# Four projections accumulated side by side while the input arrives, and four edits of order, in a layer of S5 and retention heads on one core

## The chip, the core and the metric

The kernel runs on one of the eight cores of a Trainium2 chip. The core has five engines that run side by side and meet at semaphores: TensorE (PE in the profile; its weight loads are PEld), VectorE (DVE), ScalarE (ACT), GpSimd (POOL), and SyncE (SP), which here issues almost all DMA transfers. Each engine works through its own list of instructions in the order in which the program put them there. The metric is the device time of one execution in microseconds (us), the median of several runs.

## The reference, cut to what matters

One layer of a decoder works on 256 prompt positions and 8 samples of 8 positions, 320 columns in all. Everything is float32.

```
h = rms_norm(x, norm_mix)                      # x: 320 x 2048
u, q, k, v, g = split(h @ w_in)                # five parts of 1024 columns
s5_out = glu(gelu(s5_scan(u)))                 # 64 groups of 16 channels, complex states
o = retention(rotary(q), rotary(k), v)         # 8 heads of 128
ret_out = silu(g) * group_norm(o)
x = x + concat(s5_out, ret_out) @ w_out
h2 = rms_norm(x, norm_ffn)
gate, up = split(h2 @ w_ffn_in)                # 2 x 5632 columns
x = x + (silu(gate) * up) @ w_ffn_out
y = rms_norm(x, norm_final)
```

The last states of the S5 scan and of the retention are outputs too.

## The kernel before

**Products.** All large products are tiles of 128 x 128 weights (the stationary operand) by 128 x 320 of the transposed input, summed in a PSUM tile of 128 x 320. For precision a weight tile `raw` is split into `hi` (ScalarE casts it, line 130) and `lo` = `raw` - `hi` (VectorE subtracts, line 131), and the input likewise into `xhi` and `xlo`. Each tile then takes three matmuls, `hi` by `xhi`, `hi` by `xlo`, `lo` by `xhi` (lines 141 to 143). `wload` loads weights eight tiles at a time (512 KB a DMA). A product over 2048 inputs is 16 tiles, 48 matmuls and two such loads. `raw`, `hi` and `lo` have three buffers each (in the pool `wp`; later `wp2` has four of `raw`, three of the others), so a load waits until the product three loads back has let go of its buffers.

**The front.** `x` arrives in parts of 2 to 4 of its 16 tiles while two of the 40 projections of `w_in`, u0 and u1, are summed (lines 813 to 858): `py0` and the first half of `pb0` hold their sums. Then come q and k of head 0 (`gemm("ps_p", w_in[8], ...)` into the second half of `pb0`, `proj(9)` into a tile of the pool `ps_acc`), then v. The norm of x isn't needed for these sums: it is applied where PSUM is read, by the factor `rbc`. `square_x` adds the squares of x, `finish_norm` turns the sum into `rbc`, scales the rotary tables `csr` by it, and reads out u0 and u1. The pool `ps_acc` has two tiles: a projection there waits until the one before the last has been read.

**The order.** PE and POOL run in the order in which the program is written. A clock of estimated PE time, `clk.now`, decides where a generator's next piece goes: every product advances it, `spawn` puts a piece after a delay of the table `DL` (for the chunk c of the S5 part at `T0 + PER * c`), and `run_due` emits pieces when they are due. The order on DVE, ACT and SP is set by the framework's scheduler when the program is built; `tc.high_priority(offset=...)` puts instructions forward there (`EVAC` is 1500).

**Heads and chunks.** Behind the projections run the 8 heads of retention (`head_k`: `pst` transposes k, `pss` holds the scores, VectorE multiplies them by the mask into `sm` and `smp`; `head_v`: `po` is the output, then `psr`, then `pn`) and the 8 chunks of the S5 part (`s5_chunk`: transposes `pt`, products `pb`, `pk_` and `py`). VectorE computes the S5 parameters (`s5_params`, tiles `tab`, `ecs`, `lp`) in small instructions in the first 75 us. Then come w_out, the GLU, and the feed-forward part (`ffn_in`, `ffn_out`); in the first quarter of it the retention states of the samples are updated: `states_split` copies parts of `kv` to other partitions with 16 DMAs (lines 1046 to 1055), `states_load` builds a masked product `vm` on VectorE, `states_add` multiplies on TensorE (`psu`, line 1073).

Of the kernel before, what the change touches and what calls it, by code (L numbers as in the profile page):

```python
# [12 lines left out]
F32 = mybir.dt.float32  # L13
F32R = mybir.dt.float32r
# [6 lines left out]
P = 128  # L21
# [20 lines left out]


@with_exitstack
def hybrid_kernel(ctx, tc, xT, w_in, w_out, w_glu, w_fi, w_fo, vecs, s5p, bc, x0,
                  r0, trig, masks, kdec, bmask, gq,
                  yT, s5p_o, s5s_o, rp_o, rs_o):
    nc = tc.nc
# [6 lines left out]
    def f(t):  # L55
        return t.bitcast(F32)
# [18 lines left out]
    def v(nm, i):  # L75
        return vec[:, voff[nm] + i:voff[nm] + i + 1]
# [186 lines left out]
    last_ins = {}

    def split_x(c, i0, i1):
        xr = xrs[c]
        for i in range(i0, i1):
            k = 4 * c + i
            if k == 0 or c == 3 and i % 2:
                ts(xhi[:, k], xr[:, i], v("g_mix", k), MUL)  # L270
            else:
                a_ = act.mul(xhi[:, k], xr[:, i], v("g_mix", k))
                last_ins["act"] = a_
            last_ins["dve"] = dve.scalar_tensor_tensor(xlo[:, k], xr[:, i], v("g_mix", k), f(xhi[:, k]), MUL, SUB)

    def square_x():
        for xr in xrs:
            act.activation(xr, xr, AF.Square)
        a = retp[:, 0:4]
        tt(a, a, retp[:, 4:8], ADD)  # L280
        tt(u32[:, 0:4], u32[:, 0:4], u32[:, 4:8], ADD)
        tt(a, a, u32[:, 0:4], ADD)
        tt(a[:, 0:2], a[:, 0:2], a[:, 2:4], ADD)
        tt(a[:, 0], a[:, 0], a[:, 1], ADD)
        return a[:, 0]

# [214 lines left out]
    def s5_chunk(c):  # L501
# [57 lines left out]
                    mm(0.04, pb[gs, u, NC * i:NC * i + NC], bst[us, i, gs], kst[us, 2 * (i % 2) + g],  # L559
                       start=True, stop=True, tile_position=(64 * u, 64 * g))  # L560
        pk_ = misc("pk_")
        for i in range(2):
            for q in range(2):

                mm(0.12, pk_[:, 64 * i:64 * i + 64], bl[:, q, i].rearrange("p u e h -> p (u e h)"),
                   cl[:, q, i::2, 0], start=q == 0, stop=q == 1)
        for u in range(2):
            for g in range(2):
                hs = slice(16 * g, 16 * g + 16)
                act.copy(kbd[64 * g:64 * g + 64, 2 * u:2 * u + 2, hs],  # L570
                         pk_[64 * u:64 * u + 64, 0:P].rearrange("p (i u h) -> p u i h", u=2, h=32)[:, u, :, hs])
# [222 lines left out]
    def do_g(h):  # L794
        ps = proj(11 + 4 * h)
        sg = mp.tile([P, N], F32, name="sg", tag="sg", bufs=2)
        with tc.high_priority(offset=EVAC):
# [16 lines left out]
    ws = [[], []]
    with tc.high_priority(offset=100000):
        with tc.manual_schedule(engines={mybir.EngineType.SP}):
            act.dma_start(vec, vecs)
            k0 = 0
            for b, k1 in enumerate((2, 4, 8, 12, 16)):
                c, q = k0 // 4, slice(k0 % 8, (k1 - 1) % 8 + 1)  # L820
                for i in range(2):
                    if k0 % 8 == 0:
                        raw = (wp.tile([P, 8, P], F32, name="raw", tag="raw", bufs=wpool[1][0]) if not c else
                               s5.tile([P, 8, P], F32, name="raw0", tag="bst", bufs=1) if not i else
                               mp.tile([P, 8, P], F32, name="raw1", tag="rt", bufs=1))
                        ws[i].append([raw] + [wp.tile([P, 8, P], F32R, name=n, tag=n, bufs=wpool[1][1])
                                              for n in ("hi", "lo")])
                xs = [slice(0, 1), slice(1, 2)] if not b else [slice(k0 % 4, (k1 - 1) % 4 + 1)]
                for i in range(2):
                    if i < len(xs):  # L830
                        sp.dma_start(xrs[c][:, xs[i]], xT[:, 4 * c + xs[i].start:4 * c + xs[i].stop])
                    sp.dma_start(ws[i][-1][0][:, q], w_in[i, :, k0:k1])
                if b == 2:
                    sp.dma_start(prm, s5p)
                for i in range(2):
                    raw, hi, lo = ws[i][-1]
                    if i < len(xs):
                        split_x(c, xs[i].start, xs[i].stop)
                    act.copy(hi[:, q], raw[:, q])
                    last_ins["lo"] = dve.tensor_tensor(lo[:, q], raw[:, q], f(hi[:, q]), SUB)  # L840
                k0 = k1
# [6 lines left out]
    for k0, k1 in ((0, 2), (2, 4), (4, 8), (8, 12), (12, 16)):
        for i, ps in enumerate((ps0, ps1)):
            for k in range(k0, k1):  # L850
                hi, lo = (t_[:, k % 8] for t_ in ws[i][k // 8][1:])
                pe.matmul(ps, hi, xhi[:, k], start=k == 0, stop=False)
                pe.matmul(ps, hi, xlo[:, k], start=False, stop=False)
                pe.matmul(ps, lo, xhi[:, k], start=False, stop=k == KT - 1)
                clk.now += 0.4
# [187 lines left out]
    SU = {}  # L1043

    def states_split():
        kvh, kvl = (wp.tile([P, 8, P], F32R, name=n, tag=n, bufs=3) for n in ("hi", "lo"))
        act.copy(kvh, kv)
        tt(kvl, kv, f(kvh), SUB)
        SU["k"] = [wp.tile([P, 8, P], F32R, name="hi", tag="hi", bufs=3) for _ in range(2)]
        SU["v"] = [wp.tile([P, 8, P], F32R, name="lo", tag="lo", bufs=3) for _ in range(2)]  # L1050
        for i in range(2):
            for a in range(4):
                d = slice(32 * a, 32 * a + 32)
                sp.dma_start(f(SU["k"][i][d]), f((kvh, kvl)[a // 2][64 + 32 * i:96 + 32 * i]))
                sp.dma_start(f(SU["v"][i][d]), f((kvh, kvl)[a % 2][32 * i:32 * i + 32]))
# [91 lines left out]
def _host(inp):  # L1147
# [91 lines left out]
```

## Time and profile before

| | |
|---|---|
| median of 3 runs | 1469.57 us (1468.65 to 1471.67) |
| the profiled execution | 1472.44 us, its span 1470.7 us |
| mean granted TensorE clock in it | 0.991 of full speed |
| PE, PEld, DVE, ACT, POOL busy | 98%, 97%, 58%, 41%, 7% of the span |
| PE's first matmul of a product, and its last of all | 4.73 us, 1460.2 us |

The profile is of one execution. All times below are us from the start of its span. A row of the timeline gives the start, the duration, engine, line, operation, the tiles written and read, and in brackets the idle time of the engine just before, with what ended it. Matmuls are pipelined, so that the distance of two starts tells more than the duration. PEclk is the share of the full clock of 2.4 GHz that was granted in a stretch: 1.00 or, at 1.2 GHz, 0.50.

### The profile page before, as it was taken

The numbers are of one execution on the slowest core, as the hardware profiler recorded it, in microseconds if no ns is written. First come the engines' busy times: TensorE is split into PE (matmuls) and PEld (weight loads), VectorE is DVE, ScalarE is ACT, GpSimd is POOL, SyncE is SP. The second block draws the span as 40 slices with busy tenths as digits, with TensorE's granted clock in tenths as the row PEclk, the third lists the DMA queues.
The fourth block names the chain that finished last, engine by engine and source line by source line (L and its number), as shares of the span: only waits on it lengthen the run. The fifth ranks groups of instructions, "written<-read, shape, count | busy, mean of one in ns | idle before, by whom it ended". The sixth has DMA issues, their size and how long they took to land.

```text
span 1470.7 us, 26250 instructions
## 1 busy us (share of the span) xinstructions
PE 1447.6 (98%) x10590; PEld 1430.7 (97%) x10590; DVE 851.3 (58%) x1411; ACT 606.2 (41%) x972; POOL 103.2 (7%) x228
## 2 busy tenths in 40 slices
PE   9999999999999999999999999999999999999997
PEld 8899999899999999999999999999999999999996
DVE  8987776777756755665444444444444444444454
ACT  6455555455445543333333333333333333333352
POOL 2424403200000000000000000000000000000001
PEclk9999999999999999999999999999999999999999
DMA  7445554454644475665444345444445544445543
GB/s 271 153 143 165 164 161 147 140 157 142 223 144 154 148 232 174 210 215 176 154 144 157 123 145 178 151 151 147 136 142 154 167 155 146 149 123 154 152 144 112
DMA packets 85001, 235.39 MB, mean 160 GB/s; under 512 B 16400, under 2 KB 32912, under 8 KB 84880
## 3 DMA queue, kind: packets, MB, share of 16 engines
q1 hardware_dynamic: 84736, 233.68, 50.3%
q8 instruction: 84, 1.38, 0.4%
q14 instruction: 37, 0.30, 0.1%
q10 hardware_dynamic: 144, 0.04, 0.0%
HBM read 222.63 MB, written 8.95 MB: 157 GB/s over the span
## 4 chain that ended last, share of the span: by engine, by line
PE 69%; DVE 1%; DMA 0%; issue 0%; ACT 0%; DVEq 0%; SPq 0%
PE ps_fu L143 7%; PE ps_fo L143 7%; PE ps_fo L141 7%; PE ps_fu L141 7%; PE ps_fu L142 7%; PE ps_fo L142 7%; PE ps_fg L141 7%; PE ps_fg L143 7%; PE ps_fg L142 7%; PE ps_o L142 1%; PE ps_o L141 1%; PE ps_o L143 1%; PE ps_g L142 1%; PE ps_g L143 1%; PE ps_g L141 1%; DMA raw<-w_fi 0%
## 5 line engine op out<-in xcount | busy, mean ns | idle before, releaser
L131 DVE TENSOR_TENSOR lo<-raw,hi 128x1024 fp32r<-128x1024 f32 (+1 forms) x420 | 472.7, 1126 | 391.6 <-ACT hi L130 390.8
L130 ACT CAST hi<-raw 128x1024 fp32r<-128x1024 f32 (+1 forms) x420 | 406.5, 968 | 700.7 <-PE ps_fo L142 189.2
L141 PE MATMUL ps_fg<-hhi,hi 128*128 128x320 f32 x704 | 218.3, 310 | 0.0
L142 PE MATMUL ps_fg<-hlo,hi 128*128 128x320 f32 x704 | 218.0, 310 | 0.0
L143 PE MATMUL ps_fg<-hhi,lo 128*128 128x320 f32 x704 | 218.0, 310 | 0.0
L142 PE MATMUL ps_fo<-alo,hi 128*128 128x320 f32 x704 | 217.5, 309 | 0.0
L143 PE MATMUL ps_fo<-ahi,lo 128*128 128x320 f32 x704 | 217.5, 309 | 0.0
L141 PE MATMUL ps_fo<-ahi,hi 128*128 128x320 f32 x704 | 217.5, 309 | 0.0
L143 PE MATMUL ps_fu<-hhi,lo 128*128 128x320 f32 x704 | 217.4, 309 | 0.0
L142 PE MATMUL ps_fu<-hlo,hi 128*128 128x320 f32 x704 | 217.4, 309 | 0.0
L141 PE MATMUL ps_fu<-hhi,hi 128*128 128x320 f32 x704 | 217.4, 309 | 0.0
L141 PE MATMUL ps_p<-xhi,hi 128*128 128x320 f32 x576 | 183.4, 318 | 1.2 <-DVE k__3504 L176 1.2
L142 PE MATMUL ps_p<-xlo,hi 128*128 128x320 f32 x576 | 178.9, 311 | 0.0
L143 PE MATMUL ps_p<-xhi,lo 128*128 128x320 f32 x576 | 178.9, 311 | 0.0
L142 PEld LDWEIGHTS ps_fg<-hlo,hi 128*128 128x128 f32 x704 | 133.0, 189 | 0.4
L141 PEld LDWEIGHTS ps_fg<-hhi,hi 128*128 128x128 f32 x704 | 132.9, 189 | 0.3
L143 PEld LDWEIGHTS ps_fg<-hhi,lo 128*128 128x128 f32 x704 | 133.0, 189 | 0.0
L142 PEld LDWEIGHTS ps_fu<-hlo,hi 128*128 128x128 f32 x704 | 132.4, 188 | 0.0
L143 PEld LDWEIGHTS ps_fu<-hhi,lo 128*128 128x128 f32 x704 | 132.4, 188 | 0.0
L141 PEld LDWEIGHTS ps_fu<-hhi,hi 128*128 128x128 f32 x704 | 132.4, 188 | 0.0
L141 PEld LDWEIGHTS ps_fo<-ahi,hi 128*128 128x128 f32 x704 | 132.1, 188 | 0.0
L142 PEld LDWEIGHTS ps_fo<-alo,hi 128*128 128x128 f32 x704 | 132.1, 188 | 0.0
(404 smaller groups left out, 1966.7 us busy)
## 6 DMA issues: line engine op xcount, KB each, us to landing
raw<-w_fi SPq DMA_DIRECT2D x176, 512.0 KB, 3.7
raw<-w_in SPq DMA_DIRECT2D x76, 512.0 KB, 4.2
raw<-w_fo SPq DMA_DIRECT2D x64, 512.0 KB, 3.5
raw<-w_out SPq DMA_DIRECT2D x32, 512.0 KB, 3.8
raw<-w_fo SPq DMA_DIRECT2D x64, 192.0 KB, 2.4
rt<-r SPq DMA_DIRECT2D x8, 512.0 KB, 5.4
raw<-w_glu SPq DMA_DIRECT2D x8, 512.0 KB, 3.5
raw<-r SPq DMA_DIRECT2D x8, 512.0 KB, 4.4
```

The source lines that it names most:

```text
L130: act.copy(hi[:, :m], raw[:, :m])
L131: dve.tensor_tensor(lo[:, :m], raw[:, :m], f(hi[:, :m]), SUB)
L141: pe.matmul(ps, hi, xhi[:, k], start=k == 0, stop=False)
L142: pe.matmul(ps, hi, xlo[:, k], start=False, stop=False)
L143: pe.matmul(ps, lo, xhi[:, k], start=False, stop=k == nk - 1)
```

## The change

Four outputs (u0, u1, and q and k of head 0) are summed at once while x comes in. Their weights stand in one new array `w_in4`, in which a tile k of x finds its four weight tiles side by side: a DMA of 512 KB brings the weights of all four for two tiles of x. `x` comes in parts of 1, 1, and then 2 tiles; its squares are taken part by part between the casts. The other edits: `pk_` is computed in eight matmuls of 64 x 32 outputs instead of four of 128 x 64, the three mask products of `head_k` get the priority `EVAC`, `states_split` as a whole gets the priority 6000, and the table has `nm` 0.8 instead of 7.8 (the norm's delay) and `T0` 54.6 instead of 52.6.

```diff
-    def square_x():
-        for xr in xrs:
-            act.activation(xr, xr, AF.Square)
...
+    def square_x(k0, k1):
+        xr = xrs[k0 // 4][:, k0 % 4:(k1 - 1) % 4 + 1]
+        act.activation(xr, xr, AF.Square)
...
-        for i in range(2):
-            for q in range(2):
-
-                mm(0.12, pk_[:, 64 * i:64 * i + 64], bl[:, q, i].rearrange("p u e h -> p (u e h)"),
-                   cl[:, q, i::2, 0], start=q == 0, stop=q == 1)
+        for u in range(2):
+            for i in range(2):
+                for q in range(2):
+                    mm(0.04, pk_[64 * u:64 * u + 64, 32 * i:32 * i + 32],
+                       bl[:, q, i, u].rearrange("p e h -> p (e h)"), cl[:, q, 2 * u + i, 0],
+                       start=q == 0, stop=q == 1, tile_position=(0, 64 * u))
...
-        tt(sm[:, 0:256], pss[:, 0:256], mk[:, 0:NP], MUL)
-        tt(sm[:, 256:384], pss[:, 256:384], mk[:, 0:P], MUL)
-        tt(smp[64:128, :, 0:NS], pss[64:128, 384:448].rearrange("p (b t) -> p b t", t=NS),
-           mk[64:128, NP:320].rearrange("p (b t) -> p b t", t=NS), MUL)
+        with tc.high_priority(offset=EVAC):
+            tt(sm[:, 0:256], pss[:, 0:256], mk[:, 0:NP], MUL)
+            tt(sm[:, 256:384], pss[:, 256:384], mk[:, 0:P], MUL)
+            tt(smp[64:128, :, 0:NS], pss[64:128, 384:448].rearrange("p (b t) -> p b t", t=NS),
+               mk[64:128, NP:320].rearrange("p (b t) -> p b t", t=NS), MUL)
...
-              o=2.2, u=6.0, c=10.0, n2=2.4, n2b=2.6, nm=7.8)
-    T0, PER = 52.6, 34.0
+              o=2.2, u=6.0, c=10.0, n2=2.4, n2b=2.6, nm=0.8)
+    T0, PER = 54.6, 34.0
...
+    pk0 = ps_acc.tile([P, 512], F32, name="ps_p", tag="acc", bufs=2)
+    accs = [py0[:, :N], pb0[:, 0, :N], pb0[:, 1, :N], pk0[:, :N]]
...
+    for k1 in (1, *range(2, KT + 1, 2)):
+        with tc.high_priority(offset=100000), tc.manual_schedule(engines={mybir.EngineType.SP}):
+            if k0 % 2 == 0:
+                raw, hi, lo = (wp.tile([P, 8, P], d, name=n, tag=n, bufs=3).rearrange("p (k o) m -> p k o m", o=4)
+                               for n, d in (("raw", F32), ("hi", F32R), ("lo", F32R)))
+            q = slice(k0 % 2, (k1 - 1) % 2 + 1)
+            sp.dma_start(xrs[k0 // 4][:, k0 % 4:(k1 - 1) % 4 + 1], xT[:, k0:k1])
+            sp.dma_start(raw[:, q], w_in4[:, k0:k1])
...
+            split_x(k0, k1)
+            act.copy(hi[:, q], raw[:, q])
+            last_lo = dve.tensor_tensor(lo[:, q], raw[:, q], f(hi[:, q]), SUB)
...
+        if k1 % 2 == 0:
+            accq = square_x(k1 - 2, k1)
+        for k in range(k0, k1):
+            for w_, x_ in ((hi, xhi), (hi, xlo), (lo, xhi)):
+                for i, ps in enumerate(accs):
+                    pe.matmul(ps, w_[:, k % 2, i], x_[:, k], start=k == 0 and w_ is hi and x_ is xhi,
+                              stop=k == KT - 1 and w_ is lo)
+            clk.now += 1.6
+        k0 = k1
+    ps0, ps1, pq, pk = accs
...
-    pq = gemm("ps_p", w_in[8], KT, xhi, xlo, ps=pb0[:, 1, :N])
-    pk = proj(9)
...
     def states_split():
+
+        with tc.high_priority(offset=6000):
+            states_split_()
+
+    def states_split_():
...
+    A["w_in4"] = c(A["w_in"][[0, 1, 8, 9]].transpose(1, 2, 0, 3))
```

Three places show how the built order moves. The first is TensorE's list from the first product on; `py` and the two halves of `pb` are three of the sums, `ps_p` in the changed list is the fourth. Before:

```order
L116 MATMUL warm_ps<-ones 128x512 x8
L852 MATMUL py_259<-xhi,hi 128x320
L853 MATMUL py_259<-xlo,hi 128x320
L854 MATMUL py_259<-xhi,lo 128x320
L852 MATMUL py_259<-xhi,hi 128x320
L853 MATMUL py_259<-xlo,hi 128x320
L854 MATMUL py_259<-xhi,lo 128x320
L852 MATMUL pb_260<-xhi,hi 128x320
```

and in the changed kernel:

```order
L116 MATMUL warm_ps<-ones 128x512 x8
L846 MATMUL py_152<-xhi,hi 128x320
L846 MATMUL pb_153<-xhi,hi 128x320 x2
L846 MATMUL ps_p<-xhi,hi 128x320
L846 MATMUL py_152<-xlo,hi 128x320
L846 MATMUL pb_153<-xlo,hi 128x320 x2
L846 MATMUL ps_p<-xlo,hi 128x320
L846 MATMUL py_152<-xhi,lo 128x320
L846 MATMUL pb_153<-xhi,lo 128x320 x2
L846 MATMUL ps_p<-xhi,lo 128x320
```

A tile of x now gives twelve matmuls in a row on four sums, where it gave three on one. The sums of squares (`ps_r`) come after k has been summed, two tiles into v, where they came four tiles into k.

The second is VectorE's list where head 0's q and k have been rotated: `k_<-ps_p,csr` reads the PSUM tile of k, `sg<-ps_p,rbc` reads that of g, the projection after v. Before:

```order
L176 TENSOR_TENSOR q__766<-q__766,sw 128x320
L176 TENSOR_TENSOR ecs<-tab 128x3x32
L180 SCALAR_TENSOR_TENSOR ecs<-ecs 128x3x32
L176 TENSOR_TENSOR tab<-ecs 128x64 x2
L180 SCALAR_TENSOR_TENSOR ecs<-ecs 128x2x32
L176 TENSOR_TENSOR ecs<-tab 128x2x32
L176 TENSOR_TENSOR tab<-tab 128x32
L131 TENSOR_TENSOR lo<-raw,hi 128x1024
L176 TENSOR_TENSOR k__774<-ps_p,csr 128x320
L176 TENSOR_TENSOR sw<-sw,csr 128x320
L170 TENSOR_SCALAR tab<-tab 128x32 x2
L176 TENSOR_TENSOR k__774<-k__774,sw 128x320
```

and in the changed kernel:

```order
L176 TENSOR_TENSOR q__786<-q__786,sw 128x320
L176 TENSOR_TENSOR ecs<-tab 128x3x32
L176 TENSOR_TENSOR sg<-ps_p,rbc 128x320
L180 SCALAR_TENSOR_TENSOR ecs<-ecs 128x3x32
L176 TENSOR_TENSOR tab<-ecs 128x64
L131 TENSOR_TENSOR lo<-raw,hi 128x1024
L176 TENSOR_TENSOR k__794<-ps_p,csr 128x320
L176 TENSOR_TENSOR sw<-sw,csr 128x320
L176 TENSOR_TENSOR tab<-ecs 128x64
L176 TENSOR_TENSOR k__794<-k__794,sw 128x320
```

The read of g's sum stood right behind the last row of k; now it stands ahead of the read of k's sum, with a `lo` between them.

The third is VectorE's list at the first pair of feed-forward products: `fg` and `fu` read the sums of gate and up, `hi<-lo,bmk` and `lo<-lo,bmk` build `vm` for the states of heads 0 and 1, `lo<-raw,hi` are the weights. Before:

```order
L176 TENSOR_TENSOR fg<-ps_fg,rbc_5869 128x320
L131 TENSOR_TENSOR lo<-raw,hi 128x1024
L176 TENSOR_TENSOR fu<-ps_fu,rbc_5869 128x320
L176 TENSOR_TENSOR fu<-fu,fg 128x320
L131 TENSOR_TENSOR lo<-raw,hi 128x1024
L176 TENSOR_TENSOR alo<-fu,ahi 128x320
L131 TENSOR_TENSOR lo<-raw,hi 128x1024
```

and in the changed kernel:

```order
L176 TENSOR_TENSOR fg<-ps_fg,rbc_5921 128x320
L176 TENSOR_TENSOR fu<-ps_fu,rbc_5921 128x320
L176 TENSOR_TENSOR fu<-fu,fg 128x320
L176 TENSOR_TENSOR alo<-fu,ahi 128x320
L176 TENSOR_TENSOR hi<-lo,bmk 128x512 x2
L176 TENSOR_TENSOR lo<-lo,bmk 128x512 x2
L131 TENSOR_TENSOR lo<-raw,hi 128x1024 x3
L176 TENSOR_TENSOR fg<-ps_fg,rbc_5921 128x320
```

The `lo` of the second half of the next gate weights stood ahead of `fu`; now it stands behind `alo` and the four builds. On SP the 16 DMAs of `states_split` stood one by one between weight loads; now they stand in one block behind the third `raw<-w_fi` of `wp2`, and the load of that same second half is the first one behind the block.

## Rows read from the trace of the kernel before

**Rows 1.** Waits of PE: line, waited for, us in total, times, longest

```profile
PE psu L1073 <- issue: 2.7, 1, 2.7
PE po L102 <- DVE smp L176: 2.0, 1, 2.0
...
PE ps_p L141 <- DVE k__3504 L176: 1.2, 1, 1.2
...
PE po L102 <- DVE lp L176: 0.9, 1, 0.9
PE pst L107 <- DVE k__3504 L176: 0.8, 1, 0.8
...
PE pss L102 <- ACT kbd L570: 0.5, 1, 0.5
```

**Rows 2.** Stretches: length, busy us (instructions) of PE to POOL, PEclk, DMA share, GB/s

```profile
7.60:11.00 3.40, 3.40 (x15) 3.40 (x14) 1.67 (x4) 1.42 (x4) 0.39 (x3) 0.50 0.92 311
40.50:57.90 17.40, 17.40 (x122) 17.40 (x121) 17.34 (x69) 9.42 (x14) 4.23 (x9) 1.00 0.54 174
65.60:72.50 6.90, 6.00 (x35) 5.39 (x36) 6.36 (x21) 1.65 (x5) 5.06 (x10) 0.51 0.37 106
577.60:581.10 3.50, 3.50 (x16) 3.50 (x15) 2.96 (x6) 0.46 (x1) 0.00 (x0) 0.51 0.41 146
```

**Rows 3.** Timeline of PE where one sum follows another

```profile
23.89 0.31 PE L854 MATMUL py<-xhi,lo 128*128 128x320 f32 x1
24.03 0.31 PE L852 MATMUL pb<-xhi,hi 128*128 128x320 f32 x1
```

**Rows 4.** Timeline of PE where v begins

```profile
40.54 0.31 PE L141 MATMUL ps_pv<-xhi,hi 128*128 128x320 f32 x1
...
40.98 0.83 PE L102 MATMUL ps_r<-ident,ry 128*128 128x128 f32 x6
41.57 0.39 PE L141 MATMUL ps_pv<-xhi,hi 128*128 128x320 f32 x1
```

**Rows 5.** Timeline of ACT in the first 19 us

```profile
5.91 0.56 ACT L272 ACTIVATE xhi<-u,vec 128x320 fp32r<-128x320 f32 x1 [1.92 <-DMA u<-xT]
...
18.45 0.60 ACT L839 CAST hi<-raw 128x512 fp32r<-128x512 f32 x1
```

**Rows 6.** Timeline of DVE, 43 to 56 us

```profile
43.17 0.89 DVE L176 TENSOR_TENSOR csr<-csr,rbc 128x320 f32<-128x320 f32 x2
...
53.39 1.22 DVE L131 TENSOR_TENSOR lo<-raw,hi 128x1024 fp32r<-128x1024 f32 x1
54.52 0.48 DVE L176 TENSOR_TENSOR k__774<-ps_p,csr 128x320 f32<-128x320 f32 x1
```

**Rows 7.** Timeline of PE, the transposes of head 0

```profile
57.94 0.49 PE L107 MATMUL pst<-ident,k__774 128*128 128x128 f32 x3
...
81.93 0.60 PE L107 MATMUL pn<-ident,on 128*128 128x128 f32 x4
```

**Rows 8.** The page's DMA issues: count, KB each, median us to landing

```profile
raw<-w_fi SPq DMA_DIRECT2D x176, 512.0 KB, 3.7
```

**Rows 9.** Timeline of SP's queue, the first DMA of `states_split`

```profile
525.45 0.60 SPq L1054 DMA_DIRECT2D hi<-hi  x1
```

**Rows 10.** Timeline of DVE in the first feed-forward products

```profile
531.74 0.49 DVE L176 TENSOR_TENSOR fu<-ps_fu,rbc 128x320 f32<-128x320 f32 x1 [1.38 <-PE ps_fu L143]
...
533.81 0.48 DVE L176 TENSOR_TENSOR alo<-fu,ahi 128x320 fp32r<-128x320 f32 x1
...
576.66 1.29 DVE L176 TENSOR_TENSOR lo<-lo,bmk 128x512 fp32r<-128x512 f32 x2
```

**Rows 11.** Timeline of PE, one S5 chunk's small products

```profile
131.73 0.78 PE L102 MATMUL pb<-kst,bst 64*64 64x80 f32 x32
132.44 1.10 PE L102 MATMUL pk__1772<-cl,bl 128*128 128x64 f32 x8
133.36 0.39 PE L141 MATMUL ps_p<-xhi,hi 128*128 128x320 f32 x1
```

More of the change, by code (lines that the diff above doesn't have):

```diff
@@ L44, in hybrid_kernel @@
 @with_exitstack
-def hybrid_kernel(ctx, tc, xT, w_in, w_out, w_glu, w_fi, w_fo, vecs, s5p, bc, x0,
+def hybrid_kernel(ctx, tc, xT, w_in, w_in4, w_out, w_glu, w_fi, w_fo, vecs, s5p, bc, x0,
                   r0, trig, masks, kdec, bmask, gq,
@@ L261, in hybrid_kernel, with split_x @@
     xrs = [u32[:, 0:4], u32[:, 4:8], retp[:, 0:4], retp[:, 4:8]]
[L263 to L270, printed above, removed]
-            else:
-                a_ = act.mul(xhi[:, k], xr[:, i], v("g_mix", k))
-                last_ins["act"] = a_
-            last_ins["dve"] = dve.scalar_tensor_tensor(xlo[:, k], xr[:, i], v("g_mix", k), f(xhi[:, k]), MUL, SUB)
-    def square_x():
-        for xr in xrs:
-            act.activation(xr, xr, AF.Square)
[L279 to L285, printed above, removed]
+    def split_x(k0, k1):
+        for k in range(k0, k1):
+            xr = xrs[k // 4][:, k % 4]
+            if k == 0:
+                ts(xhi[:, k], xr, v("g_mix", k), MUL)
+            else:
+                act.mul(xhi[:, k], xr, v("g_mix", k))
+            dve.scalar_tensor_tensor(xlo[:, k], xr, v("g_mix", k), f(xhi[:, k]), MUL, SUB)
+    def square_x(k0, k1):
+        xr = xrs[k0 // 4][:, k0 % 4:(k1 - 1) % 4 + 1]
+        act.activation(xr, xr, AF.Square)
+        if k1 == 8:
+            tt(u32[:, 0:4], u32[:, 0:4], u32[:, 4:8], ADD)
+        elif k1 == 12:
+            tt(u32[:, 0:4], u32[:, 0:4], retp[:, 0:4], ADD)
+        elif k1 > 12:
+            a = u32[:, 0:2]
+            tt(a, a, u32[:, 2:4] if k1 == 14 else retp[:, 6:8], ADD)
+            if k1 == 14:
+                tt(a, a, retp[:, 4:6], ADD)
+            else:
+                tt(a[:, 0], a[:, 0], a[:, 1], ADD)
+        return u32[:, 0]
     NE = 8
@@ L570, in s5_chunk @@
                 act.copy(kbd[64 * g:64 * g + 64, 2 * u:2 * u + 2, hs],
-                         pk_[64 * u:64 * u + 64, 0:P].rearrange("p (i u h) -> p u i h", u=2, h=32)[:, u, :, hs])
+                         pk_[64 * u:64 * u + 64, 0:64].rearrange("p (i h) -> p i h", h=32)[:, :, hs])
         pvs = [pb[:, u, 0:4 * NC].rearrange("p (r q t) -> p r q t", r=2, q=2) for u in range(2)]
@@ L812, in hybrid_kernel @@
     act.activation(warm, ones[:, 0:1], AF.Silu)
[L814 to L841, printed above, removed]
@@ L842, in hybrid_kernel @@
-    with tc.issue_after(last_ins["lo"].ins):
-        dt_ = s5_step()
     py0 = ps_y.tile([P, 512], F32, name="py0", tag="y", bufs=1)
     pb0 = ps_b.tile([P, 2, 512], F32, name="pb0", tag="pb", bufs=1)
-    ps0, ps1 = py0[:, :N], pb0[:, 0, :N]
     keep_warm(8)
[L848 to L855, printed above, removed]
@@ L856, in hybrid_kernel @@
-    with tc.issue_after(last_ins["act"].ins), tc.issue_after(last_ins["dve"].ins):
-        accq = square_x()
+    pk0 = ps_acc.tile([P, 512], F32, name="ps_p", tag="acc", bufs=2)
+    accs = [py0[:, :N], pb0[:, 0, :N], pb0[:, 1, :N], pk0[:, :N]]
+    with tc.high_priority(offset=100000), tc.manual_schedule(engines={mybir.EngineType.SP}):
+        act.dma_start(vec, vecs)
+    k0 = 0
+    for k1 in (1, *range(2, KT + 1, 2)):
+        with tc.high_priority(offset=100000), tc.manual_schedule(engines={mybir.EngineType.SP}):
+            if k0 % 2 == 0:
[4 more added lines that the diff above has]
+            sp.dma_start(raw[:, q], w_in4[:, k0:k1])
+            if k1 == 6:
+                sp.dma_start(prm, s5p)
+            split_x(k0, k1)
+            act.copy(hi[:, q], raw[:, q])
+            last_lo = dve.tensor_tensor(lo[:, q], raw[:, q], f(hi[:, q]), SUB)
+        if k1 == 6:
+            with tc.issue_after(last_lo.ins):
+                dt_ = s5_step()
+        if k1 % 2 == 0:
+            accq = square_x(k1 - 2, k1)
+        for k in range(k0, k1):
+            for w_, x_ in ((hi, xhi), (hi, xlo), (lo, xhi)):
[4 more added lines that the diff above has]
+        k0 = k1
```

## The prediction, made before the changed kernel ran

> **What bounds the kernel now.** The page's first part comes first: TensorE is busy for 98% of the span, and its clock is granted at 0.991. So only TensorE's idle time and its time at half clock can be won. One tile's three matmuls run from 40.54 to 40.98 [rows 4]: 0.147 us each, 7.04 us for a product of 48. I read the places where TensorE departs from that.
>
> The start. The first matmul of a product is at 4.73, and v begins at 40.54 [rows 4]. Between them lie 4 x 48 = 192 matmuls, 28.2 us, and the first six `ps_r`, about the 0.6 us of the second six (40.98 to 41.57). 4.73 + 28.2 + 0.6 = 33.5: 7.0 us are lost, since two sums give 96 matmuls for 16 tiles of x and x comes in slower than that. In 7.6 to 11.0 TensorE also runs at 0.50 of the clock while 311 GB/s come in [rows 2].
>
> The list of waits [rows 1] gives the rest: `po` waits for `smp` (2.0) and `lp` (0.9) at 63 to 66.5; `pss` 0.5 at 98.8; a projection and `pst` wait for a rotated k (1.2 and 0.8) at 268; `psu` 2.7, ending at 576.84, put down to "issue", where the program's order shows `hi`, `lo` and `vm` of the states as what it needs.
>
> A wait costs more than itself. After the `po` waits the clock is 0.51 for 6.9 us, after `psu` 0.51 for 3.5 us [rows 2]: 3.4 and 1.7 us of TensorE's time. I take the same 1.7 behind the two waits at 268, 2.0 together, and none behind the 0.5 at 98.8.
>
> Last, VectorE. From 40.5 to 57.9 it is busy 17.34 of 17.40 us [rows 2]: there an end moves only by what stands in its list.
>
> **A. Start to the first `pn`.** *The sums.* Tile 0 gives twelve matmuls from about 4.73. Tile 1 of x and its four weight tiles (416 KB together) come behind it; before, two tiles of x with their weights were the unit. `xhi` of tile 1 waited for its DMA until 5.91 [rows 5]. The weights for it are 256 KB in place of 128 KB a tile for two tiles; with 311 GB/s I set their landing 0.9 later, about 7.0, and the cast of 128x512 adds 0.60 [rows 5]: 7.65. Twelve at half clock, 24 x 0.147 = 3.5: 11.2. From there 14 tiles x 12 x 0.147 = 24.7: the four sums end at 35.8. They need 832 KB per two tiles in 3.52 us, 242 GB/s (1 KB = 1024 bytes), below the 311 that the trace shows. ScalarE's share of two tiles (casts, `xhi`, squares) is some 2.7 us, VectorE's some 3.1, both under 3.5; so the moved squares and casts cost nothing, and some 0.8 and 0.4 us in each 3.5 if that cover failed, 6 and 3 us in all. Before, the same point is 40.54 less 0.6 of `ps_r` inside, 39.9: 4.1 earlier.
>
> *The read of k.* The new order spends some of it. `ps_r` comes two tiles into v, at 36.7, the second `ps_r` fourteen tiles into it, at 42.3; before, the second was at 40.98 and `csr` at 43.17 [rows 4, 6]. So `csr` comes at about 44.5, later than before. From there to the end of k's read I count in VectorE's list 7 reads or products of 128x320 at 0.40, two `csr` at 0.40, some 15 small ones at 0.15 and three `lo` at 1.13 (53.39 to 54.52 [rows 6]), with gaps 9.7: 54.1. TensorE has done v, two `ps_r` and g by 35.8 + 7.0 + 1.2 + 7.0 = 51.0, and u2 needs the tile that held k. It waits 3.1 us. The least is 2.4: the read of `sg` needs the end of g, and behind it come two small ones (0.3), `lo` 1.13 and k's read 0.48, whenever the sums end. The most I take is 4.1, with `csr` one us later. Half a clock follows, 1.7. Before, k's read began at 54.52, ahead of the read of g, and TensorE did not wait.
>
> *Then to `pn`.* u2 from 54.1 gives 18 matmuls (2.6) + 1.7 until `pst` at 58.4; it was at 57.94 [rows 7]. From there to `pn` at 81.93 it took 24.0. The priority puts the mask products ahead of the parameters, so the 2.9 of `po`'s waits and 3.0 of the 3.4 of half clock should go: 18.1, `pn` at 76.5. **Gain 5.4.**
>
> **B. `pss` at 98.8.** It now stands ahead of `pk_`, with `kbd` ready: **0.5**.
>
> **C. The wait at 268.** The read of k stood behind the chunk's mask products on VectorE and stands ahead of them now: 1.2 + 0.8 + 1.7 = **3.7**; nothing, if VectorE is late for another reason.
>
> **D. `states_split`.** 2.7 + 1.7 = 4.4 go. But its 16 DMAs now form one block on SP, 0.60 us each in issue [rows 9], and a load stands behind them. The first eight wait for buffers of the first gate product's first half, the others for its end. `fu` is read at 531.74 when the first up product ends [rows 10], so that gate product ended 7.0 earlier, at 524.5. 524.5 + 8 x 0.60 = 529.3; then the second half of the next gate's weights is issued, lands 3.7 later [rows 8] at 533.0, and is cast by 534.1 to 534.6. Its `lo` stands behind `fu`, `alo` (533.81 before [rows 10], 533.7 at best now) and four builds of `vm`, 1.29 for two [rows 10], 2.5 for four: 536.2, with its own 1.13 at 537.3. TensorE began that product at 531.5 and needs this `lo` 24 matmuls and two later, at 535.2. A new wait of 2.1 + 1.7 of clock: 3.8. **Net 0.6**; 4.4 if the builds find a gap, about -1 if the block issues later by 1.6.
>
> **E. `pk_`.** Eight records with 128 columns of weights take 0.92 us (132.44 to 133.36) and become sixteen with 64. `pb`'s 32 records, on a quarter of the array, take 0.71 (131.73 to 132.44) [rows 11]: 0.022 each, four side by side 0.089. Sixteen at 0.022 are 0.4, 0.5 less; at 0.089, 1.4, 0.5 more. `pk_` runs two halves side by side, between these: I take 0, with -4 to +4 us for eight chunks. The Trainium skill ("TensorE: Matmul & The Clock Gate", section "LDWEIGHTS (loading the stationary operand)") says that a load's time goes with its columns: by that sixteen loads of half the columns take what eight took, and this term would stay 0. The sum stands without it.
>
> The new `nm` and `T0` move pieces of equal work; their effect on the norm is in A. A later chunk is covered by the head products between.
>
> **The sum.** 5.4 + 0.5 + 3.7 + 0.6 + 0 = 10.2. The profiled execution takes 1472.44, so 1462.2. It is 2.9 above the median of the runs shown; I carry the difference to the median: 1469.57 - 10.2 = **1459.4**.
>
> **The rivals.** *R1: the block of D hides.* If the `lo` behind the block is in time, 3.8 more: 1455.6. For it: VectorE is nearly idle between the products there, and the cast may be early. Against it: DMA, `fu` and builds all stand ahead in fixed lists. 0.20.
>
> *R2: the wait at 268 stays, or one like it comes up in another head.* Each head reads k by the same list, and the whole order of VectorE is moved: 3.7 less, 1463.1. For it: one head of eight lost this before. 0.25.
>
> *R3: the change brings nothing.* VectorE is full to 57.9 [rows 2], and if it stays the bound until `pn`, and C stays too, 0.5 + 0.6 are left: 1468.5. Against it: what it computes behind k is moved behind the masks, not only shifted. 0.07.
>
> *R4, slower: the four sums never get the full clock.* Twelve matmuls go round over four PSUM tiles, where each tile gave its sum three in a row. If the clock then stays at half until the sums end, 168 matmuls cost 24.7 more. The wait for k drops to its least (0.7 less) and most of A's 5.4 is consumed: 10.2 - 24.7 + 0.7 + some 1.7 of a clock that can't fall further = -12; 1481 to 1482. It ends slower from about 70 matmuls at half clock on. Against it: a change of the sum from `py` to `pb` costs 23.89 to 24.03 [rows 3], 0.14, no more than within a sum. The Trainium skill (the same page, section "A second HAM failure mode: psum-queue depth-cycling") tells of a kernel whose clock went to and fro as it cycled through PSUM banks; by that rule R4 holds. The traced change of tiles speaks against it so far. 0.03.
>
> **How the numbers follow.** 0.45 for the forecast, 0.20, 0.25, 0.07, 0.03 for the rivals. The bounds of k's wait (-0.7, +1.0), of E (4 either way, likelier within 2) and of D widen each by some 2 us. From R1 less 1.6 to R2 plus 2.9: 1454 to 1466, which leaves out R3, R4 and the tails of E, under 0.2. About 0.2%, 2.9 us, is what a measurement here can tell from no change: faster below 1466.6, slower above 1472.5. Forecast, R1 and R2 lie below but for their tails (0.03), R3 within with part of these, R4 and two mishaps together above: 0.87, 0.08, 0.05.
>
> **What would show it.** A: twelve matmuls a tile at 0.147 from 11.2, v at 35.8, a wait of some 3 us for k's read at 51 to 54, `pst` near 58.4, `pn` near 76.5, no wait of `po`. C: none at 268. D: no `psu` wait; a wait for `lo` at 535, of some 2 us. E: sixteen `pk_` records in some 0.9 us. Wrong would make it: gaps between the tiles of x (the DMA or the casts are the bound), a half clock past 11.2, a wait in a later head, or a `pk_` round of 1.4 us.

## The result, and the profile after

The changed kernel takes 1474.91 us (median of 9 runs, 1474.05 to 1476.02), the kernel before 1470.78 in as many runs beside it (1468.65 to 1472.64): a ratio of 1.0030, 95% interval 1.0021 to 1.0039. It is slower by some 4 us where 10 less were forecast. The profiled execution takes 1475.36 us, 2.92 more than that of before. One of the ten executions of e1 below took 2013.88 us, and its median is that of the other nine.

The waits of TensorE after, the view of [rows 1]:

```profile
PE py L102 <- DVE xp L176: 6.2, 1, 6.2
PE ps_p L141 <- DVE sg L176: 3.2, 1, 3.2
PE py L846 <- DVE xhi L170: 3.2, 1, 3.2
PE ps_p L141 <- DVE k__3502 L176: 1.3, 1, 1.3
...
PE ps_fg L141 <- ACT hi L130: 1.1, 1, 1.1
PE ps_fg L143 <- DVE lo L131: 0.7, 1, 0.7
PE ps_p L143 <- DVE lo L131: 0.7, 1, 0.7
PE ps_p L141 <- DVE q__1098 L176: 0.5, 1, 0.5
```

Of the six waits of [rows 1] five are gone; that of a projection for a rotated k has 1.3 where it had 1.2. The two largest that no step of the prediction had are the first and the third line.

**The start.** VectorE's and GpSimd's timelines in the first 9 us:

```profile
3.29 4.69 DVE L170 TENSOR_SCALAR xhi<-u,vec 128x320 fp32r<-128x320 f32 x1 [3.29 <-DMA vec<-vecs]
8.01 0.55 DVE L270 SCALAR_TENSOR_TENSOR xlo<-u,vec,xhi 128x320 fp32r<-128x320 f32 x1
```

```profile
3.05 1.20 POOL L319 MEMSET xp<- 128x640 f32 x2
4.19 0.20 POOL L319 MEMSET kbd<- 128x128 f32 x1
4.34 1.17 POOL L319 MEMSET ush<- 128x1280 f32 x1
5.45 2.27 POOL L319 MEMSET cl<- 128x1280 f32 x2
7.65 0.11 POOL L464 MEMSET tab<- 128x8 f32 x1
7.69 0.11 POOL L465 MEMSET tab<- 128x8 f32 x1
```

The first `xhi` of VectorE takes 4.69 us and ends at 7.98, just after GpSimd's last memset (7.80). So TensorE begins at 8.13 where it began at 4.73. This row and later ones of its timeline:

```profile
8.13 0.39 PE L846 MATMUL py<-xhi,hi 128*128 128x320 f32 x1 [3.23 <-DVE xhi L170]
...
37.89 0.31 PE L141 MATMUL ps_pv<-xhi,hi 128*128 128x320 f32 x1
...
56.71 0.60 PE L141 MATMUL ps_p<-xhi,hi 128*128 128x320 f32 x1 [3.23 <-DVE sg L176]
...
60.92 0.49 PE L107 MATMUL pst<-ident,k__794 128*128 128x128 f32 x3
...
78.86 0.89 PE L107 MATMUL pn<-ident,on 128*128 128x128 f32 x3
...
375.25 2.43 PE L102 MATMUL py<-xp,cl 128*32 128x80 f32 x64 [6.23 <-DVE xp L176]
```

The four sums take 29.8 us (8.13 to 37.89). v begins 2.7 earlier than in [rows 4], `pn` comes 3.1 earlier than in [rows 7]. Up to here the change is a gain.

**The last chunk.** The last row is the loss. VectorE's list ahead of that `py`:

```profile
368.32 1.29 DVE L176 TENSOR_TENSOR v<-w,tab 128x512 f32<-128x512 f32 x2
369.53 0.48 DVE L176 TENSOR_TENSOR sg<-ps_p,rbc 128x320 f32<-128x320 f32 x1
369.94 1.22 DVE L131 TENSOR_TENSOR lo<-raw,hi 128x1024 fp32r<-128x1024 f32 x1
371.07 1.69 DVE L176 TENSOR_TENSOR r4a<-retp,r4a 128x320 fp32r<-128x320 f32 x4
372.68 0.48 DVE L176 TENSOR_TENSOR r4b<-retp,r4b 128x320 fp32r<-128x320 f32 x1
373.08 0.49 DVE L176 TENSOR_TENSOR retp<-retp,sg 128x320 f32<-128x320 f32 x1
373.48 1.29 DVE L176 TENSOR_TENSOR r4b<-retp,r4b 128x320 fp32r<-128x320 f32 x3
374.69 0.74 DVE L176 TENSOR_TENSOR xp<-v,v 128x252 f32<-128x252 f32 x2
```

`v` is ready at 369.6, but `xp`, which TensorE waits for, stands behind the splits of the heads' outputs for w_out (`r4a`, `r4b`, line 947), which TensorE needs only after that `py`. Before, `xp` stood right behind `v`, ahead of the splits:

```profile
368.17 1.29 DVE L176 TENSOR_TENSOR v<-w,tab 128x512 f32<-128x512 f32 x2
...
369.50 0.75 DVE L176 TENSOR_TENSOR xp<-v,v 128x252 f32<-128x252 f32 x2
370.16 1.22 DVE L131 TENSOR_TENSOR lo<-raw,hi 128x1024 fp32r<-128x1024 f32 x1
371.30 1.69 DVE L176 TENSOR_TENSOR r4a<-retp,r4a 128x320 fp32r<-128x320 f32 x4
```

TensorE also has less to do in between. From the chunk's `pb` to its `py` it took 12.8 us before, with 75 matmuls of projections behind `pk_`:

```profile
359.24 0.78 PE L102 MATMUL pb<-kst,bst 64*64 64x80 f32 x32
...
372.05 0.74 PE L102 MATMUL py<-ush,kbd 128*32 128x320 f32 x8
372.61 1.29 PE L102 MATMUL py<-xp,cl 128*32 128x80 f32 x64
```

In the changed kernel it takes 9.2, with 51 of them:

```profile
359.05 0.78 PE L102 MATMUL pb<-kst,bst 64*64 64x80 f32 x32
...
368.27 0.74 PE L102 MATMUL py<-ush,kbd 128*32 128x320 f32 x8
```

Within that wait the clock falls, in the view of [rows 2]:

```profile
56.70:60.00 3.30, 3.29 (x12) 3.30 (x13) 3.30 (x14) 1.15 (x3) 0.47 (x1) 0.50 0.89 259
374.10:380.80 6.70, 5.55 (x76) 5.26 (x77) 5.55 (x19) 1.47 (x3) 0.00 (x0) 0.50 0.81 304
541.50:544.90 3.40, 2.70 (x17) 2.44 (x18) 2.74 (x3) 2.10 (x2) 0.00 (x0) 1.00 0.91 347
```

TensorE is busy in 5.55 of the 6.7 us at 0.50, which costs 2.8: with the wait 9.0, nearly all of the gain that was forecast. (The expectations below take 3.4, half of the whole stretch.) The two waits for `hi` and `lo` at 541 cost no clock in this execution.

### The profile page after: what moved, and what is told of

It reads as the page before. It is cut to its first block, busy times and chain, and to the rows that moved or that the text cites. A ratio compares the mean times of both kernels' runs of the same rounds, so it can differ in the third digit from the quotient of the medians.

```text
span 1473.6 us, 26372 instructions
## 1 busy us (share of the span) xinstructions
PE 1444.0 (98%) x10654; PEld 1426.7 (97%) x10654; DVE 854.3 (58%) x1405; ACT 607.6 (41%) x973; POOL 101.8 (7%) x228
## 4 chain that ended last, share of the span: by engine, by line
PE 69%; DVE 1%; issue 0%; ACT 0%; DVEq 0%
PE ps_fo L143 7%; PE ps_fo L142 7%; PE ps_fu L143 7%; PE ps_fu L142 7%; PE ps_fu L141 7%; PE ps_fo L141 7%; PE ps_fg L143 7%; PE ps_fg L141 7%; PE ps_fg L142 7%; PE ps_o L142 1%; PE ps_o L141 1%; PE ps_o L143 1%; PE ps_g L142 1%; PE ps_g L143 1%; PE ps_g L141 1%; DVE x L176 0%
## 5 line engine op out<-in xcount | busy, mean ns | idle before, releaser
L130 ACT CAST hi<-raw 128x1024 fp32r<-128x1024 f32 (+1 forms) x416 | 402.0, 967 | 680.1 <-PE ps_fo L142 189.3
L141 PE MATMUL ps_p<-xhi,hi 128*128 128x320 f32 x560 | 178.4, 318 | 5.2 <-DVE sg L176 3.2
L143 PE MATMUL ps_p<-xhi,lo 128*128 128x320 f32 x560 | 173.9, 311 | 0.7 <-DVE lo L131 0.7
L142 PE MATMUL ps_p<-xlo,hi 128*128 128x320 f32 x560 | 173.6, 310 | 0.0
```

The costliest lines, as they stand in the source:

```text
L130: act.copy(hi[:, :m], raw[:, :m])
L143: pe.matmul(ps, lo, xhi[:, k], start=False, stop=k == nk - 1)
```

## The experiments

Theory: two causes, VectorE's `TENSOR_SCALAR` held by GpSimd's memsets at the start, and the place of `xp` behind the splits in VectorE's list. Rivals: the first is a late input; the second comes from a late VectorE; or one of the repairs (priorities, `pk_`) does harm by itself. All times below are medians with their ratio to the kernel before on the same chip.

**The start.** e1 changes the operation:

```diff
-                ts(xhi[:, k], xr, v("g_mix", k), MUL)
+                dve.scalar_tensor_tensor(xhi[:, k], xr, v("g_mix", k), ones[:, 0:1].to_broadcast([P, N]), MUL, MUL)
```

> The changed kernel, but VectorE makes xhi of tile 0 with a SCALAR_TENSOR_TENSOR (x by the factor by ones) in place of the TENSOR_SCALAR that took 4.69 us and ended when GpSimd's memsets ended. Theory (a TENSOR_SCALAR of 32 bits waits for GpSimd, the three-operand form doesn't): xhi takes about 0.55 us, the first matmul of a product comes at about 4.6 in place of 8.13, and what follows is 3.4 us earlier up to the read of sg at 56: from there VectorE decides, so that between 1 and 3.4 us reach the end, 1471.5 to 1474. Rival (VectorE is held by a late input or by every operation beside memsets): xhi still takes over 4 us, 1474.9.

1473.02 us, ratio 1.0015 (1.0006 to 1.0025). e6 keeps the operation and moves GpSimd's memsets:

```diff
-    for t_ in (*d0s, *xps, kbd, ush, *cls_):
-        pool.memset(t_, 0.0)
...
+            if k1 == 1:
+                pool.tensor_scalar(kbd[:, 0], f(xhi[:, 0, 0:32]), 0.0, None, MUL)
+                for t_ in (*d0s, *xps, kbd, ush, *cls_):
+                    pool.memset(t_, 0.0)
```

> The changed kernel with VectorE's TENSOR_SCALAR for xhi of tile 0 as it was, and GpSimd's memsets of d, xp, kbd, ush and cl behind it: a small product of GpSimd that reads xhi stands ahead of them. Theory (the memsets held the TENSOR_SCALAR): it takes 0.5 us or less in place of 4.69, the first matmul of a product comes at 4.2 to 4.8, the time as in the run with the three-operand form, 1473.2. Rival (this operation is slow there for another reason): over 3 us still, 1474.9.

1473.24 us, ratio 1.0020 (1.0011 to 1.0029). VectorE's first operation in e1:

```profile
3.44 0.55 DVE L267 SCALAR_TENSOR_TENSOR xhi<-u,vec,ones 128x320 fp32r<-128x320 f32 x1 [3.44 <-DMA vec<-vecs]
```

and in e6, the same operation as in the changed kernel:

```profile
3.37 0.39 DVE L170 TENSOR_SCALAR xhi<-u,vec 128x320 fp32r<-128x320 f32 x1 [3.37 <-DMA vec<-vecs]
```

Both ways the long wait is gone, the first product matmul is at 4.67 and 4.70, and 1.7 to 1.9 us reach the end. `pn` comes at 75.39 in e1. What held VectorE were the memsets (e6), and the operation with two tensor operands was not held beside the same memsets (e1). The Trainium skill ("SBUF — State Buffer", section "Who interferes with whom") says that a VectorE operation in a two-port mode and a GpSimd operation lock each other out for a whole instruction. The 4.69 us beside the memsets and the 0.39 without them agree with it, though no run shows in which mode the operation was; and in the changed kernel VectorE lost to memset after memset, until GpSimd had none left.

e16 puts ScalarE in VectorE's place for this tile in the kernel before:

```diff
-            if k == 0 or c == 3 and i % 2:
+            if c == 3 and i % 2:
```

> The kernel before with xhi of tile 0 by ScalarE. Theory (there too the TENSOR_SCALAR waited for GpSimd, 1.18 us in its profile where 0.39 is what it takes): the first matmul of a product 0 to 0.5 earlier; the stretch behind waits for x, so 0 to 0.7 less, and the spread of its times (1467.5 to 1474) smaller if some executions waited 4.7 us: none over 1472. Rival (no such executions before): same time, same spread.

1470.81 us, 0.9997 (0.9985 to 1.0009), times from 1467.65 to 1473.79. The rival holds: nothing is won before, and the spread there comes from elsewhere.

**The last chunk.** e2 and e9 change T0 (54.6), e3 gives `xp` of the last chunk a priority, e10 takes the old `pk_`, e13 changes its planned cost only:

```diff
-    T0, PER = 54.6, 34.0
+    T0, PER = 50.6, 34.0
```

> The changed kernel with T0 50.6 in place of 54.6, by which VectorE's list has xp of the last chunk ahead of the splits r4a and r4b again. Theory (the wait of 6.2 at 375 and the 6.8 us of half clock behind it come from that order): both go, 1474.9 - 6.2 - 3.4 = 1465.3. Rival (the chunk is late on VectorE because of the four sums or the mask products): a wait of 4 us or more stays, 1473 to 1475.

```diff
+        with (tc.high_priority(offset=EVAC) if c == 7 else ExitStack()):
             tt(xp[:, 0, :, 1:NCP], t[0][:, 0, :, 0:NCP - 1], t[1][:, 1, :, 0:NCP - 1], SUB)
             tt(xp[:, 1, :, 1:NCP], t[0][:, 1, :, 0:NCP - 1], t[1][:, 0, :, 0:NCP - 1], ADD)
```

> The changed kernel with the priority EVAC for the two products that write xp in the last chunk, nothing else; in VectorE's list they stand ahead of r4a. Theory (those splits ahead of xp are most of the wait of 6.2): xp is done at about 371.8 in place of 375.3, the wait falls to 2.8, the half clock to one stretch of 3.4 us: 1474.9 - 3.4 - 1.7 = 1469.8. Rival (what stands ahead of v, not behind it, makes it late): the wait stays over 5, 1474.9.

```diff
-    T0, PER = 54.6, 34.0
+    T0, PER = 52.6, 34.0
```

> The changed kernel with T0 52.6, as it was before the change. Its list on VectorE still has the second product of xp behind r4a and r4b, though the last chunk now begins 15 matmuls of projections earlier. Theory (the place of xp in VectorE's list is what counts): a wait of 5 to 6.2 stays at 375, 1474 to 1475. Rival (the two us of T0 are the cause): the wait goes, 1465 to 1468.

```diff
-        for u in range(2):
-            for i in range(2):
-                for q in range(2):
-                    mm(0.04, pk_[64 * u:64 * u + 64, 32 * i:32 * i + 32],
...
+        for i in range(2):
+            for q in range(2):
+                mm(0.12, pk_[:, 64 * i:64 * i + 64], bl[:, q, i].rearrange("p u e h -> p (u e h)"),
...
```

> The changed kernel with pk_ in four matmuls of 128 x 64 again, at their old cost in the planner's clock; T0 stays 54.6. By that cost the last chunk stands 3 matmuls earlier, and VectorE's list has both products of xp ahead of r4a. Theory (place in the list): the wait at 375 falls to about 2.6, half clock to one stretch, as with the priority for xp: 1469.8, with 0.6 more for pk_ itself (0.92 us a chunk in place of 0.84): 1470.4. Rival (pk_ has nothing to do with it): 1474.9 to 1475.5.

```diff
-                    mm(0.04, pk_[64 * u:64 * u + 64, 32 * i:32 * i + 32],
+                    mm(0.06, pk_[64 * u:64 * u + 64, 32 * i:32 * i + 32],
```

> The changed kernel with one number changed: the planned cost of each of the eight pk_ matmuls 0.06 in place of 0.04, so that a chunk's pk_ costs 0.48 in the planner's clock, as in the kernel before. TensorE's list then has the last chunk where the run with the old pk_ has it (54 matmuls ahead of py), but VectorE's list still has the second product of xp behind r4b. Theory (the place of xp in VectorE's list sets the wait): a wait of 3 us or more at the last py stays, 1472 to 1474. Rival (the chunk's place on TensorE does, or the form of pk_ cost the time): the first gives 1466.2 as with the old pk_, the second 1474.9.

| run | us | ratio (95%) | waits at the last `py` |
|---|---|---|---|
| e2, T0 50.6 | 1466.57 | 0.9963 (0.9949 to 0.9977) | none |
| e3, `xp` first | 1469.80 | 0.9994 (0.9985 to 1.0004) | 2.6 |
| e9, T0 52.6 | 1473.80 | 1.0023 (1.0014 to 1.0033) | 1.1 + 3.1 |
| e10, old `pk_` | 1466.84 | 0.9972 (0.9961 to 0.9983) | 0.6 |
| e13, cost 0.06 | 1473.08 | 1.0013 (1.0003 to 1.0022) | 1.1 + 4.7 |

e3 came out at its forecast: nothing but the place of `xp` is changed there, and 5 us come back. e2 is 1.3 slower than its theory. e9 is just below its range, with 4.2 of wait where 5 to 6.2 were expected. e10 is 3.6 faster than its theory, which had a wait of 2.6 left. e13 is the sharpest: TensorE's list has the chunk where e10 has it, but VectorE's list still has the second product of `xp` behind `r4b`:

```profile
366.50 0.41 DVE L176 TENSOR_TENSOR xp<-v,v 128x252 f32<-128x252 f32 x1
...
370.38 1.29 DVE L176 TENSOR_TENSOR r4b<-retp,r4b 128x320 fp32r<-128x320 f32 x3
371.58 0.41 DVE L176 TENSOR_TENSOR xp<-v,v 128x252 f32<-128x252 f32 x1
```

and the wait stays, where in e10 both stand ahead:

```profile
364.35 0.74 DVE L176 TENSOR_TENSOR xp<-v,v 128x252 f32<-128x252 f32 x2
365.00 1.22 DVE L131 TENSOR_TENSOR lo<-raw,hi 128x1024 fp32r<-128x1024 f32 x1
366.14 1.70 DVE L176 TENSOR_TENSOR r4a<-retp,r4a 128x320 fp32r<-128x320 f32 x4
```

TensorE's rows there, of e13 and then of e10:

```profile
367.06 0.35 PE L102 MATMUL py<-xp,cl 128*32 128x80 f32 x8 [1.07 <-DVE xp L176]
372.14 2.10 PE L102 MATMUL py<-xp,cl 128*32 128x80 f32 x56 [4.74 <-DVE cl L176]
```

```profile
364.90 1.51 PE L102 MATMUL py<-xp,cl 128*32 128x80 f32 x64 [0.62 <-ACT r4a L945]
```

In both, 54 matmuls stand between `pk_` and `py`, and `py` comes 9.7 us after `pb`; the wait is 5.8 in e13 and 0.6 in e10. So the list on VectorE makes that difference. The profile puts 4.7 of e13 and 3.1 of e9 down to `cl`, the row behind `xp` in that list, and the 0.6 of e10 to `r4a`; but TensorE goes on 0.14 us after the `xp` that it needs has ended each time (372.00 to 372.14, 372.52 to 372.66, 364.76 to 364.90).

TensorE's side counts beside it. e3 has the list right and keeps the 51 matmuls, and a wait of 2.6 and a stretch of half clock stay. Of the 24 matmuls that the changed kernel lacks there, T0 takes 15 (e9 has 66) and the planned cost of `pk_` 3 (e13); the other 6 are not assigned.

Which edit turned VectorE's list is not shown. The old T0 alone (e9) and the old planned cost alone (e13) leave the second product of `xp` behind the splits; T0 50.6 (e2) or the old `pk_` with its old cost (e10) puts both ahead. e2, e10 and e13 had the short start in their profiles (`xhi` 1.17, 1.19 and 1.28 us), so some 2 us of their times beside the changed kernel may be the start.

**The start and the last chunk together.** e5 is e2 with `act.mul` for tile 0, e15 is e10 with it:

```diff
-            if k == 0:
-                ts(xhi[:, k], xr, v("g_mix", k), MUL)
-            else:
-                act.mul(xhi[:, k], xr, v("g_mix", k))
+            act.mul(xhi[:, k], xr, v("g_mix", k))
```

> The changed kernel with T0 50.6 and with xhi of tile 0 made by ScalarE like all others. Theory (two separate causes, the start and the last chunk): their gains add up, 1466.6 less 1.7 to 3.4, so 1463.2 to 1464.9. Rival (what is won at the start is lost again at the read of sg and k, which VectorE's list sets): 1466.6.

1465.03 us, 0.9962 (0.9948 to 0.9977): just above the theory's range and 1.5 below e2, but the ratios of the two are the same (0.9963 in e2), so that a gain over e2 is not shown.

> The changed kernel with the old pk_ and xhi of tile 0 by ScalarE: both causes taken away with T0 54.6 left. The run with the old pk_ alone had the short start in its profile (first matmul before 5 us, xhi 1.19 us) and times from 1463.9 to 1468.3. Theory (VectorE's TENSOR_SCALAR waits in some executions and not in others): without it the times stay in the lower half, median 1464 to 1465.5, none over 1467. Rival (that spread comes from elsewhere): 1466.8, up to 1468.

1465.09 us, 0.9952 (0.9937 to 0.9967), 1463.49 to 1465.57, where e10 had 1463.92 to 1468.32. That the upper half of e10's times were long starts fits, with 4 times against 7; it was not traced run by run.

**The repairs by themselves.** e4 is the changed kernel, and e7 is e5, without the priority of `states_split`; e11 is e5 without that of the mask products:

```diff
-        with tc.high_priority(offset=6000):
-            states_split_()
+        states_split_()
```

> The changed kernel without the priority 6000 of states_split. Theory (it took away the wait of 2.7 and half clock of 1.7 at psu and put waits of 1.1 and 0.7 for hi and lo at 541 in their place): psu waits again, those go, 1474.9 + 4.4 - 1.8 = 1477.5. Rival (psu no longer waits, since its pieces stand at other places now): 1473.1.

> As the run with T0 50.6 and xhi by ScalarE, and without the priority 6000 of states_split. Theory (with the priority, hi and lo of the second gate product come late, which cost 2.3 + 0.5 of waits and 3.4 of half clock in the run with T0 50.6, more than the wait of 2.7 and 1.7 at psu that it takes away): 1.7 less than its neighbour, 1461.5 to 1463. Rival (my forecast: the priority is worth 0.6): 0.6 more than its neighbour or above.

e4 takes 1474.75 (1.0025, 1.0015 to 1.0034), e7 1465.15 (0.9963, 0.9949 to 0.9977): as their neighbours, between the two forecasts each time. In both traces `psu` waits 2.7 again and the waits for `hi` and `lo` of the second gate product are gone. The priority exchanges one for the other.

```diff
-        with tc.high_priority(offset=EVAC):
+        if True:
             tt(sm[:, 0:256], pss[:, 0:256], mk[:, 0:NP], MUL)
...
```

> As the run with T0 50.6 and xhi by ScalarE, and without the priority of the three mask products. Theory (that priority took away the waits of po for lp and smp, 2.9, and 3.4 of half clock): they come back, 1465.0 + 3 to 6.3 = 1468 to 1471.3. Rival (VectorE had done the parameters by then anyway, since TensorE comes later relative to it): 1465.0.

1463.22 us (0.9953, 0.9937 to 0.9970), not slower than e5, and `po` waits for nothing. My theory falls: in e5's order VectorE has the masks done in time without it.

**A faster version.** e8 is e5 with k's sum in another tile, so that u2 has one that is free:

```diff
-    pk0 = ps_acc.tile([P, 512], F32, name="ps_p", tag="acc", bufs=2)
+    pk0 = ps_v.tile([P, 4, P], F32, name="po", tag="po", bufs=1).rearrange("p a b -> p (a b)")
...
-        yield DL["k"]
+        yield DL["k"] + (4.0 if h == 0 else 0.0)
...
-        yield DL["v"] + (3.0 if h == 0 else 0.0)
+        yield DL["v"] + (7.0 if h == 0 else 0.0)
```

> As the run with T0 50.6 and xhi by ScalarE, and k of head 0 is summed in the PSUM tile of po, which is idle until 62, so that the product u2 need not wait for k's read; head 0's transposes come 4.0 later. Theory (the wait of 2.7 to 3.2 for the read of sg and k and the half clock behind it come from the two tiles of ps_acc): no wait at 53, 3 to 4.5 less than its neighbour, 1459 to 1461. Rival (VectorE is the bound there and the wait moves to pst): as its neighbour, 1463 to 1465.

1466.43 us (0.9976, 0.9964 to 0.9987). The wait for `sg` is gone, and its rival is right in kind, though the time lies above its range and the wait is not at `pst`: it comes at the next thing that VectorE makes, the first chunk's `bl`:

```profile
PE pt L107 <- DVE bl L176: 4.9, 2, 4.7
```

e12 gives that chunk more time (T0 54.6, PER 33.4), e14 drops the mask priority as well:

> xhi of tile 0 by ScalarE, k of head 0 summed in the PSUM tile of po and head 0's transposes 4.0 later, as before, but T0 54.6 with PER 33.4: the first chunk's transposes pt stand behind pn, for VectorE to finish what they need, and the last chunk is due when it was with T0 50.6 and PER 34. Theory (the wait of 4.7 of pt at 81.6 and the half clock behind it took back what k's tile had won): both go, 1466.4 - 4.7 - 3.4 = 1458.3 to 1461. Rival (VectorE is the bound up to 82 and a wait of the same size comes at the next thing): 1465 to 1466.5.

1462.57 us, 0.9945 (0.9930 to 0.9960): 1.6 to 4.3 above its theory. In its trace the wait for `bl` is gone and `q` of head 1 is waited for (2.2).

> The fastest one so far (xhi of tile 0 by ScalarE, k of head 0 in po's tile, T0 54.6, PER 33.4) without the priority of the mask products. Theory (that priority is worth nothing, and its neighbour without it had 1463.2 beside 1465.0): 1460.8 to 1462.6. Rival (it is worth something where head 0 comes earlier): 1464 to 1466, with a wait of po.

1461.82 us, 0.9928 (0.9911 to 0.9944): the fastest, 9 us below the kernel before, though not told apart from e12. In its trace `po` waits again, 3.4, put down to `lp`, where e12 with the priority has the 2.2 for `q`: one wait stands for the other, and the time shows no gain of the priority.

## Why the prediction was wrong, step by step

**The step that failed** is the sentence "The new `nm` and `T0` move pieces of equal work; their effect on the norm is in A. A later chunk is covered by the head products between." The pieces are equal, their place and their order are not. Between `pk_` and `py` of the last chunk stand no head products, only projections, and with the new plan 51 of their matmuls are left of 75: 3.6 us of cover are gone (12.8 to 9.2 us from `pb` to `py`). On VectorE the scheduler puts `r4a` and `r4b` ahead of this `xp`, so that from the start of `pb` to the end of `xp` it takes 16.4 us in place of 11.0; e3, with `xp` ahead of them, has 12.8. Together that cost 6.2 + 2.8 = 9.0 of the profiled execution. That these two make the wait is shown (e2, e3, e10 and e13); which edit turned VectorE's list stays open. The built order shows the place, but the prediction doesn't compare it.

**A.** "Tile 0 gives twelve matmuls from about 4.73" failed: 8.13, since the same `TENSOR_SCALAR` took 4.69 us in place of 1.18. It cost 1.7 to 1.9 us at the end (e1, e6). The rest held: the sums took 29.8 where 31.1 were worked out, and with the short start of e1 v begins at 35.27, where 35.8 was worked out; the wait at the read of `sg` and k was 3.2 and its half clock 3.3 us, as sized (3.1); in the twelve other traces with k in that tile it was 1.1 to 3.3, in seven of them without a fall of the clock. In e1 `pn` came at 75.39, where 76.5 was forecast; the changed kernel has 78.86. That the mask priority was needed for this isn't borne out: e11, which is e5 without it, has no wait of `po` and `pn` at 74.78.

**B and C.** `pss` waits no more at 98.8, but `lo` and `q` of head 1 cost 0.7 + 0.5 at 82 to 87. Of the two waits at 268 (2.0) and the clock (1.7) one of 1.3 is left, without a fall of the clock: 2.4 of 3.7, as rival R2 had it in kind. Less than that reached w_out: from `pn` to the first matmul of w_out e15 takes 291.6 us where the kernel before took 291.9.

**D.** The wait that I forecast for `lo` at 535, 2.1, came as 1.1 for `hi` and 0.7 for `lo` at 541, and the cast was late too. The clock fell behind it in some traces (e5, e6) and not in others. The net gain was forecast at 0.6; measured it is -0.2 (e4) and 0.1 (e7), which can't be told from none.

**E.** `pk_`'s sixteen records take 0.84 us (359.76 to 360.60) where eight took 0.92: 0.6 less in all, within the bounds. What it cost lies in the order (e10 beside e13).

With both causes taken away 6.1 of the 10.2 are left in the medians (e15, 1465.09 beside 1471.21). Between the traced executions it is 7.8 (1472.44 to 1464.66). In that trace A gave 6.5 (`pn` at 75.42), 1.1 more than forecast. From there to w_out 0.3 is left of the 4.2 of B and C, with waits of 0.7 and 0.5 at 79 to 84, 0.5 at 261 and 0.6 at the last `py`; at the start of w_out 1.0 is lost, 0.7 of it waiting for `r4a`. D gave 2.2 there, with waits of 1.0 and 0.7 and no fall of the clock, though the medians of e4 and e7 show no such gain. Small terms on both sides make up the rest; I can't assign them one by one.

R1 and R3 did not happen. R4 did not either: from 12.2 on the clock was 1.00 through some 175 matmuls that went round over four tiles. The forecast of a gain was right about the front and wrong about the kernel.

## What to carry to other kernels

Where a table or a planned cost changes, compare the built order on every engine through to the end, the last piece above all: count what still stands in it to cover a wait (75 matmuls before, 51 after). A priority that helps one consumer puts everything else behind it; ask who waits for what it overtakes (`r4a` over `xp`). In a start that waits for a single VectorE operation, keep GpSimd quiet or give the operation to ScalarE; here that gave 1.7 us in the changed kernel (e6) and nothing in the kernel before (e16).

## What the hardware showed that I had not expected

One instruction of 0.39 us took 1.2 to 1.3 or 4.4 to 4.7 us beside the same memsets. Starts at 3.30 to 3.40 gave the short form (before, e2, e10, e13), starts at 3.25, 3.29 and 3.62 the long one (after, e3, e4, e9). In the short form `ush`'s memset took 1.35 in place of 1.17, as if it had let VectorE in. What decides is open.
